# Weight tiles that meet 256 columns: high part 192 bytes further on modulo 256 than the low part

## The chip, the cores and the metric

The kernel runs on one core of one Trainium2 chip. The metric is device time in microseconds (us) of the whole kernel, the median of three runs. TensorE (PE) does the matrix products, and its weight loads are listed apart (PEld); VectorE (DVE) and ScalarE (ACT) do the elementwise work; GpSimd (POOL) does some of it and issues some DMAs; SyncE (SP) issues the rest. All tiles lie in the on-chip memory, 128 partitions high; an address below is a byte offset within each partition.

## The reference

A decoder trunk of two layers over 512 tokens of width 1024, in float32. Each layer is

```python
h = h + 0.5 * swiglu(rmsnorm(h, nw[0]), ffn_w_in[i, 0], ffn_w_out[i, 0])
h = h + mixer(rmsnorm(h, nw[1]))          # layer 0: retention, layer 1: forgetting attention
h = h + 0.5 * swiglu(rmsnorm(h, nw[2]), ffn_w_in[i, 1], ffn_w_out[i, 1])
h = h + sigmoid(rmsnorm(h, nw[3]) @ ple_w_gate[i]) * (p[i] @ ple_w_proj[i])
```

and a last rmsnorm. `swiglu(x)` is `(silu(g) * u) @ w_out` with `g, u` the two halves of `x @ w_in`, and 2816 hidden columns. So there are four such FFNs, two mixers and two gated per-layer inputs (PLE).

## The kernel before

**Products in three parts.** Every float32 operand is held as a high part (`hi`, rounded to the type that TensorE multiplies) and a low part (`lo`, the rest). A product is three matmuls: high by high, high by low, low by high. The weights are the stationary operand, 128 columns of 4 bytes (512 bytes per partition), loaded anew for each matmul; the activations are the moving operand, 512 or 256 columns (2048 or 1024 bytes per partition).

**Two widths.** Most products have 512 moving columns: retention, attention, the FFNs' output matrices and the first PLE (lines 323 to 325 and 702 to 704). With 256 columns run:

- the FFNs' input matrices in a seven-product (Strassen-like) form, line 508. Of the 22 column blocks of an FFN, 20 go this way. A block is seven products of 12 matmuls: eight with the high part (four slices of the weight, each against the high and the low half of an activation), then four with the low part. Two of the seven take the weight as loaded, `pair.t`, a `w8` tile (products `b11` and `t4`); five take sums of its quarters, tiles `s12`, `s34` and `a12`. The order over blocks is: `b11`, two sum products of the next block; then `t4` and three sum products of the one before.
- the other two blocks of each FFN (`plain`, line 543), with `w8` tiles (in the third FFN the first block's come from `s34` and `a12` buffers): high, high, low, then the next tile.
- the second PLE, which runs in two halves of 256 tokens (lines 323 to 325 with 256 columns): high, high, low for each slice of the weight.

An FFN is: two `plain` blocks, then three chunks of 6, 8 and 8 blocks; after each chunk eight output blocks with 512 columns add up. So a chunk's 256-column stretch follows a 512-column one twice per FFN, and follows `plain` once.

**Weights.** A `Weights` object loads each weight by a DMA from SP's queue into a `wraw` buffer, two tiles ahead of use; ACT copies it into the high part, DVE or POOL subtracts to the low part (lines 83, 84), or ACT negates and a DMA of POOL's queue adds (lines 125 to 127). The `w8` tiles have three buffers (`wpool`); for the second PLE a further pool of five (`wkept`) takes the last weights so that both halves can use them. TensorE's order is written out by hand.

**Addresses.** What matters for the change is where the operands of one matmul begin modulo 256 bytes. In the built program:

| buffer | role | begins at, modulo 256 |
|---|---|---|
| `unit_a` to `unit_d` | moving operand of all these products | 32 |
| `w8` in `wpool` (high and low part, 4096 bytes apart) | stationary | 32 |
| `s12`, `s34`, `a12` (all parts) | stationary | 224 |
| `w8` in `wkept` (high and low part) | stationary | 224 |

A slice of a weight begins a multiple of 512 bytes further on, and a half of an activation 1024, so all slices share these values.

Of the kernel before, what the change touches and what calls it, by code (L numbers as in the profile page):

```python
# [12 lines left out]
F32R = mybir.dt.float32r  # L13
# [4 lines left out]
P = 128  # L18
# [9 lines left out]
LOOKAHEAD = 2  # L28
# [7 lines left out]
class Pair:  # L36
# [3 lines left out]
    def __init__(self, ffn, q, r):  # L40
        self.ffn, self.q, self.r, self.direct = ffn, q, r, False
# [13 lines left out]
class Weights:  # L55
# [3 lines left out]
    def __init__(self, tc, raw_pool, pool):  # L59
        self.tc, self.nc, self.raw_pool, self.pool = tc, tc.nc, raw_pool, pool  # L60
        self.plan, self.ready, self.used = [], [], 0
        self.low = self.nc.vector
        self.limit, self.spare = None, []
        self.look, self.placed = LOOKAHEAD, {}
        self.sum_pool, self.open_ffn, self.pairs_used = None, None, 0
        self.ahead, self.behind = 0, ()

# [6 lines left out]
    def load(self, src):  # L74
        raw = self.raw_pool.tile([P, 1024], F32, name="wraw")
        self.nc.sync.dma_start(out=raw[:, : src.shape[1]], in_=src)
        return raw

    def split(self, raw, hi, lo, src=None):
        if self.low is None and src is not None:  # L80
            self.negated(raw, hi, lo, src)
            return
        self.nc.scalar.copy(hi, raw)  # L83
        self.low.tensor_tensor(out=lo, in0=raw, in1=hi.bitcast(F32), op=ALU.subtract)  # L84

    def chunk(self, src):
        n = src.shape[1]
        raw = self.load(src)
        if id(src) in self.placed:
            hi, lo = (t.rearrange("p a c -> p (a c)") for t in self.placed.pop(id(src))())  # L90
            self.split(raw, hi, lo)
            return hi, lo
        if self.spare:
            tiles = [self.spare.pop(0)() for _ in range(4)]
            for i in range(2):
                self.split(raw[:, 512 * i : 512 * (i + 1)], tiles[i], tiles[2 + i])
            return Halves(tiles[0:2]), Halves(tiles[2:4])
        t = self.pool.tile([P, 2, 1024], F32R, name="w8")
        self.split(raw[:, :n], t[:, 0, :n], t[:, 1, :n], src)
        return t[:, 0, :], t[:, 1, :]  # L100

    def emit_parts(self, parts):

        nc = self.nc
        halves = lambda ap: ap.rearrange("p (h c) -> p h c", h=2)
        tiles = [
            (
                self.raw_pool.tile([P, 1024], F32, name="wraw"),
                self.pool.tile([P, 2, 1024], F32R, name="w8"),
            )  # L110
            for _ in range(2)
        ]
        for j0, j1 in parts:
            cs = slice(j0 * P, j1 * P)
            for src, (raw, t) in zip(self.plan, tiles):
                r, hi, lo = (halves(x)[:, :, cs] for x in (raw, t[:, 0, :], t[:, 1, :]))
                nc.sync.dma_start(out=r, in_=halves(src)[:, :, cs])
                nc.vector.tensor_copy(hi, r)
                nc.vector.tensor_tensor(out=lo, in0=r, in1=hi.bitcast(F32), op=ALU.subtract)
            yield  # L120
        self.ready += [(t[:, 0, :], t[:, 1, :]) for _, t in tiles]

    def negated(self, raw, hi, lo, src):

# [4 lines left out]
    def first(self, pair):  # L129

        pair.raw = self.load(pair.q)
        pair.t = self.pool.tile([P, 2, 1024], F32R, name="w8")
        hi, lo = pair.t[:, 0, :], pair.t[:, 1, :]
        if pair.direct:
            self.split(pair.raw, hi, lo)
        else:
            self.negated(pair.raw, hi, lo, pair.q)
# [61 lines left out]
def trunk(ctx, tc, a):  # L199
# [16 lines left out]
    W = Weights(tc, wraw, wpool)  # L216
# [5 lines left out]
    ffn_src = []  # L222
    for i in range(4):
        ins = [Pair(i, a["ffn_w_in"][i, m, 0], a["ffn_w_in"][i, m, 1]) for m in range(NF)]
        chunks = CHUNKS[i]
        outs = [[a["ffn_w_out"][i, m][:, k0 * P : k1 * P] for m in range(KB)] for k0, k1 in chunks]
        for m in [PLAIN[i]] + [k1 + 1 for _, k1 in chunks[:-1]]:
            ins[m].direct = ins[m + 1].direct = True
        ffn_src.append((ins, outs))
    ret_qk = [[a["ret_qk"][c] for c in (2 * h, 2 * h + 1, 8 + 2 * h, 9 + 2 * h)] for h in range(RH)]  # L230
    ret_v = [[a["ret_v"][h][:, c * 1024 : (c + 1) * 1024] for c in range(4)] for h in range(RH)]
    ret_g = [[a["ret_g"][4 * h + c] for c in range(4)] for h in range(RH)]
# [3 lines left out]
    fox_o = [[a["fox_o"][h, c] for c in range(4)] for h in range(2)]  # L236
    ple_g = [[a["ple_gate"][l, m] for m in range(KB)] for l in range(2)]
    ple_p = [[a["ple_proj"][l, c] for c in range(2)] for l in range(2)]

    def plan_ffn(i):  # L240
        ins, outs = ffn_src[i]
        at = PLAIN[i]
        for pair in ins[:at]:
            W.plan += [pair.q, pair.r]
        for (k0, k1), cs in zip(CHUNKS[i], outs):
            upto = min(k1 + 1, NF)
            W.plan += ins[at:upto] + cs
            at = upto
# [61 lines left out]
    def split(src, hi, lo, scale=None):  # L310

        if scale is None:
            high = nc.scalar.copy(hi, src)
            low = nc.vector.tensor_tensor(out=lo, in0=src, in1=hi.bitcast(F32), op=ALU.subtract)  # L314
        else:
            high = nc.scalar.activation(hi, src, AF.Identity, scale=scale)
            low = nc.vector.scalar_tensor_tensor(
                out=lo, in0=src, scalar=scale, in1=hi.bitcast(F32), op0=ALU.mult, op1=ALU.subtract
            )
        return high, low  # L320

    def mm3(out, wh, wl, xh, xl, first, last):
        nc.tensor.matmul(out, wh, xh, start=first, stop=False)  # L323
        nc.tensor.matmul(out, wh, xl, start=False, stop=False)  # L324
        nc.tensor.matmul(out, wl, xh, start=False, stop=last)  # L325
# [18 lines left out]
    class Norm:  # L344
# [9 lines left out]
        def halves(self, b):  # L354
            if self.forms is not None:
                return self.quarters(b)
            hi, lo = self.unit(), self.unit()
            split(h[b], hi, lo, self.gain[:, b : b + 1])
            self.hi.append(hi)
            self.lo.append(lo)  # L360
# [144 lines left out]
    def product(out, w, c, forms, name, first=False):  # L505

        xs = [form[name] for form in forms]
        add = lambda w, x, start, stop: nc.tensor.matmul(  # L508
            out, w, x, start=start, stop=stop, skip_group_check=True
        )  # L510
        for j, (xh, xl) in enumerate(xs):
            wh = w[:, 0, c + j * P : c + (j + 1) * P]
            add(wh, xh, first and j == 0, False)
            add(wh, xl, False, False)
        for j, (xh, xl) in enumerate(xs):
            add(w[:, 1, c + j * P : c + (j + 1) * P], xh, False, j == 3)

    def ffn(i, n, nxt, stack, apool, meanwhile=None):

# [32 lines left out]
        def one(m):  # L552
            pair, g, u = live[m]
            product(g[:, c0], pair.t, 0, n.forms, "b11", True)
            product(g[:, c1], pair.s[0], 0, n.forms, "t1")
# [107 lines left out]
    class OutBoth:  # L663
# [5 lines left out]
        def add(self, i, m):  # L669
            srcs, yhi, ylo = self.parts[i]  # L670
            if (i, m // 2) not in self.ws:
                self.ws[i, m // 2] = W.take(srcs[m // 2])
            wh, wl = self.ws[i, m // 2]
            for k in range(4):
                ks = slice((4 * (m % 2) + k) * P, (4 * (m % 2) + k + 1) * P)
                mm3(self.banks[m], wh[:, ks], wl[:, ks], yhi[k], ylo[k], i == 0 and k == 0, i == 1 and k == 3)
# [560 lines left out]
    norms[4].early = True  # L1237
    first = W.emit_parts(((0, 1), (1, 2), (2, 4)))
    next(first)
    load_x(1, 2)  # L1240
    load_x(2, 4)
# [15 lines left out]
    def ffn_ple(i, l, n, mid, nxt, stack, apool, parts):  # L1257
        phi, plo = [], []

        def load():  # L1260
            pv = a["pT"][l].rearrange("(b p) t -> b p t", p=P)
            for b in range(2):
                t1 = temp()
                nc.sync.dma_start(out=t1, in_=pv[b])
                phi.append(unit(uc))
                plo.append(unit(uc))
                split(t1, phi[b], plo[b])

        ffn(i, n, mid, stack, apool, load)
        stack = open_ffn(i + 1) if i < 3 else None  # L1270
        ple(l, mid, nxt, phi, plo, parts)
        return stack
# [101 lines left out]
```

## Time and profile before

| what | value |
|---|---|
| median of three runs | 2192.59 us (2189.26 to 2194.67) |
| the profiled execution | 2193.35 us, span 2191.5 us |
| mean granted TensorE clock | 0.994 |
| PE busy | 2142.5 us, 98% of the span, 13525 matmuls |
| DVE, ACT, POOL busy | 66%, 55%, 22% |
| matmuls of line 508 / line 543 | 6720 / 768 |

A busy PE is not one at its best: the matmuls overlap, and a duration in the listings runs from an instruction's start to its modelled end. What a matmul costs in a dense stretch is the distance from one start to the next. This is read from the timeline, whose rows give a start in us, a duration, the engine, the line, the operands and the count of equal instructions merged: the difference of two starts over the matmuls in between. In names, `bank<-unit_b,w` is a matmul with moving operand `unit_b` and stationary operand `w8` (the listings cut buffer numbers off, `s12` and `s34` read `s`, `a12` reads `a`).

### The profile page before, as it was taken

Reading aid. Unit: us, or ns where it says so; the run is one execution under the profiler, and the core shown is the slowest. Engines: PE = TensorE matmul, PEld = TensorE weight load, DVE = VectorE, ACT = ScalarE, POOL = GpSimd, SP = SyncE. Lnnn points to the kernel's source line nnn. Section 1 sums busy time; section 2 is a strip of 40 time slices with the busy share of each in tenths; the row PEclk is TensorE's granted clock in tenths of the full one; section 3 lists DMA queues with packets and bytes.
Section 4 is the critical chain, followed back from the end, with each engine's and each line's share of the span. In section 5 each row is a group of like instructions: output and inputs, shape, how many; then the busy total and the mean of one; then the engine's idle time right before and its main releaser. Section 6 shows DMA issues by size and latency. Waiting matters only on the chain.

```text
span 2191.5 us, 34456 instructions
## 1 busy us (share of the span) xinstructions
PE 2142.5 (98%) x13525; PEld 1927.9 (88%) x13525; DVE 1454.5 (66%) x2629; ACT 1202.4 (55%) x2027; POOL 472.6 (22%) x354
## 2 busy tenths in 40 slices
PE   8999999999999999999998999999999999999997
PEld 7999997888888798989988999898788899999987
DVE  8686766352533677767758687775675696777765
ACT  7465553433333574745556556464787774655544
POOL 0010003444344000101142011012334200100055
PEclk9999999999999999999999999999999999999999
DMA  5465562222222244746523555463622144654631
GB/s 174 124 167 148 140 164 97 82 95 77 94 77 87 77 128 132 177 119 152 144 94 97 129 160 149 137 167 105 152 81 88 67 125 114 161 154 139 155 106 40
DMA packets 85315, 267.08 MB, mean 122 GB/s; under 512 B 9360, under 2 KB 12944, under 8 KB 85152
## 3 DMA queue, kind: packets, MB, share of 16 engines
q1 hardware_dynamic: 63328, 209.78, 28.2%
q0 software_dynamic: 20592, 54.01, 14.6%
q8 instruction: 106, 1.74, 0.3%
q10 hardware_dynamic: 1232, 1.09, 0.1%
q14 instruction: 57, 0.47, 0.1%
HBM read 262.71 MB, written 2.13 MB: 121 GB/s over the span
## 4 chain that ended last, share of the span: by engine, by line
PE 85%; DVE 6%; ACT 4%; DMA 2%; issue 2%; POOL 1%; SPq 0%; ACTq 0%; DVEq 0%; POOLq 0%
PE bank L508 33%; PE bank L325 14%; PE bank L323 14%; PE bank L324 13%; PE bank L543 4%; PE bank L703 2%; PE bank L702 2%; PE bank L704 2%; DMA wraw<-in_ffn_w_in 1%; ACT p L1006 1%; DVE w L84 1%; ACT p L1008 1%; ACT w L83 1%; DVE tlo L314 1%; PE bank L337 0%
## 5 line engine op out<-in xcount | busy, mean ns | idle before, releaser
L83 ACT CAST w<-wraw 128x1024 fp32r<-128x1024 f32 (+1 forms) x240 | 243.4, 1021 | 420.0 <-PE bank L325 254.9
L325 PE MATMUL bank<-unit_a,w 128*128 128x512 f32 x736 | 287.2, 390 | 4.3 <-DVE w L84 2.6
L323 PE MATMUL bank<-unit_a,w 128*128 128x512 f32 x736 | 288.5, 392 | 1.9 <-ACT w L83 1.6
L324 PE MATMUL bank<-unit_a,w 128*128 128x512 f32 x736 | 286.7, 390 | 0.2 <-DVE unit_a L314 0.2
L84 POOL TENSOR_TENSOR w<-wraw,w 128x1024 fp32r<-128x1024 f32 x93 | 226.8, 2442 | 259.3 <-ACT w L83 246.8
L83 ACT CAST s<-sums 128x512 fp32r<-128x512 f32 x320 | 191.8, 617 | 153.4 <-DVE sums L157 107.4
L325 PE MATMUL bank<-unit_d,w 128*128 128x512 f32 (+1 forms) x712 | 268.2, 377 | 4.6 <-DVE w L84 4.6
L323 PE MATMUL bank<-unit_d,w 128*128 128x512 f32 (+1 forms) x712 | 269.3, 378 | 3.2 <-ACT w L83 1.6
L324 PE MATMUL bank<-unit_d,w 128*128 128x512 f32 (+1 forms) x712 | 268.0, 376 | 1.8 <-DVE unit_d L314 1.8
L84 DVE TENSOR_TENSOR s<-sums,s 128x512 fp32r<-128x512 f32 x320 | 214.1, 685 | 75.8 <-ACT s L83 75.3
L127 POOL DMA_DIRECT2D a<-in_ffn_w_in x80 | 70.3, 878 | 643.4 <-ACT a L126 422.0
L84 DVE TENSOR_TENSOR w<-wraw,w 128x1024 fp32r<-128x1024 f32 (+1 forms) x147 | 173.3, 1184 | 19.5 <-ACT w L83 19.3
L508 PE MATMUL bank<-unit_b,s 128*128 128x256 f32 x880 | 184.4, 276 | 0.7 <-DVE bank L565 0.7
L508 PE MATMUL bank<-unit_d,s 128*128 128x256 f32 x1140 | 178.4, 276 | 0.0
L508 PE MATMUL bank<-unit_a,s 128*128 128x256 f32 x1260 | 175.0, 276 | 1.4 <-ACT unit_a L387 0.9
L604 DVE SCALAR_TENSOR_TENSOR tmp<-bank,rows 128x512 f32<-128x512 f32 x96 | 66.0, 689 | 164.9 <-PE bank L325 163.7
L325 PEld LDWEIGHTS bank<-unit_a,w 128*128 128x128 f32 x736 | 138.1, 188 | 35.5 <-DVE w L84 4.3
L323 PEld LDWEIGHTS bank<-unit_a,w 128*128 128x128 f32 x736 | 138.2, 188 | 32.2 <-ACT w L83 3.5
L324 PEld LDWEIGHTS bank<-unit_a,w 128*128 128x128 f32 x736 | 138.2, 188 | 28.5 <-DVE unit_a L314 0.5
L325 PEld LDWEIGHTS bank<-unit_d,w 128*128 128x128 f32 x712 | 134.3, 189 | 30.7 <-DVE w L84 6.6
L323 PEld LDWEIGHTS bank<-unit_d,w 128*128 128x128 f32 x712 | 134.4, 189 | 30.2 <-ACT w L83 3.3
L508 PEld LDWEIGHTS bank<-unit_a,s 128*128 128x128 f32 x1260 | 158.0, 188 | 1.8 <-ACT unit_a L387 1.1
(292 smaller groups left out, 4787.9 us busy)
## 6 DMA issues: line engine op xcount, KB each, us to landing
wraw<-in_ffn_w_in SPq DMA_DIRECT2D x174, 512.0 KB, 4.3
wraw<-in_ffn_w_out SPq DMA_DIRECT2D x64, 512.0 KB, 4.7
w<-in_ffn_w_in POOLq DMA_DIRECT2D x56, 512.0 KB, 5.4
a<-in_ffn_w_in POOLq DMA_DIRECT2D x80, 256.0 KB, 6.3
wraw<-in_ffn_w_out SPq DMA_DIRECT2D x32, 384.0 KB, 3.7
wraw<-in_ret_qk SPq DMA_DIRECT2D x16, 512.0 KB, 3.5
wraw<-in_ret_v SPq DMA_DIRECT2D x16, 512.0 KB, 3.6
wraw<-in_ret_g SPq DMA_DIRECT2D x16, 512.0 KB, 3.5
```

The source lines that it names most:

```text
L83: self.nc.scalar.copy(hi, raw)
L84: self.low.tensor_tensor(out=lo, in0=raw, in1=hi.bitcast(F32), op=ALU.subtract)
L127: self.nc.gpsimd.dma_start(out=lo, in_=src, accum_op=ALU.add)
L323: nc.tensor.matmul(out, wh, xh, start=first, stop=False)
L324: nc.tensor.matmul(out, wh, xl, start=False, stop=False)
L325: nc.tensor.matmul(out, wl, xh, start=False, stop=last)
L508: add = lambda w, x, start, stop: nc.tensor.matmul(out, w, x, start=start, stop=stop, skip_group_check=True)
L543: nc.tensor.matmul(o[:, HALVES[t]], x[:, ks], y, start=k == t == q == 0, stop=k == KB - 1 and q == 2, skip_group_check=True,)
L604: nc.vector.scalar_tensor_tensor(out=t1, in0=o, scalar=-0.5, in1=n.r, op0=ALU.mult, op1=ALU.mult)
L702: nc.tensor.matmul(os[t], xh, wh[:, js], start=k == 0, stop=False)
L703: nc.tensor.matmul(os[t], xh, wl[:, js], start=False, stop=False)
L704: nc.tensor.matmul(os[t], xl, wh[:, js], start=False, stop=k == KB - 1)
```

## The change

Tiles for weights in a set `narrow` (the input weights of all four FFNs, and the gate and projection weights of the second PLE) place their high part 48 elements, 192 bytes, into the tile; the low part follows 1024 + 16 elements later. All `w8` tiles get 64 elements (256 bytes) longer, 8448 bytes in place of 8192. By the built program:

| buffer | high, modulo 256 | low, modulo 256 |
|---|---|---|
| `w8` in `wpool`, narrow | 32 -> 224 | 32 -> 32 |
| `w8` in `wkept` (all narrow) | 224 -> 160 | 224 -> 224 |
| `w8` in `wpool`, other | 32 -> 32 | 32 -> 32 |

Buffers that are allocated behind `wpool` move by 768 bytes, so their place modulo 256 stays (modulo 512 it moves by 256). The matmuls whose stationary operand changes its place are 1280 of line 508 (the high parts of `b11` and `t4`), 448 of line 543, and 256 of the second PLE (96 from 32 to 224, 160 from 224 to 160). The instructions of every engine, their order and their waits are the same in both programs: only addresses differ.

```diff
+    def wide(self, src):
+
+        at = 48 if id(src) in self.narrow else 0
+        t = self.pool.tile([P, 2112], F32R, name="w8")
+        return t[:, at : at + 1024], t[:, at + 1024 + (at and 16) :][:, :1024]
...
-        t = self.pool.tile([P, 2, 1024], F32R, name="w8")
-        self.split(raw[:, :n], t[:, 0, :n], t[:, 1, :n], src)
-        return t[:, 0, :], t[:, 1, :]
+        hi, lo = self.wide(src)
+        self.split(raw[:, :n], hi[:, :n], lo[:, :n], src)
+        return hi, lo
...
-        pair.t = self.pool.tile([P, 2, 1024], F32R, name="w8")
-        hi, lo = pair.t[:, 0, :], pair.t[:, 1, :]
+        pair.t = hi, lo = self.wide(pair.q)
...
+    for ins, _ in ffn_src:
+        W.narrow |= {id(x) for pair in ins for x in (pair.q, pair.r)}
...
+    W.narrow |= {id(x) for x in ple_g[1] + ple_p[1]}
...
     def product(out, w, c, forms, name, first=False):
 
         xs = [form[name] for form in forms]
+        both = w if isinstance(w, tuple) else (w[:, 0, :], w[:, 1, :])
...
         for j, (xh, xl) in enumerate(xs):
-            wh = w[:, 0, c + j * P : c + (j + 1) * P]
+            wh = both[0][:, c + j * P : c + (j + 1) * P]
             add(wh, xh, first and j == 0, False)
             add(wh, xl, False, False)
         for j, (xh, xl) in enumerate(xs):
-            add(w[:, 1, c + j * P : c + (j + 1) * P], xh, False, j == 3)
+            add(both[1][:, c + j * P : c + (j + 1) * P], xh, False, j == 3)
```

`emit_parts`, which loads the very first two weights, takes its tiles from `wide` in the same way.

More of the change, by code (lines that the diff above doesn't have):

```diff
@@ L63, in __init__ @@
         self.limit, self.spare = None, []
-        self.look, self.placed = LOOKAHEAD, {}
+        self.look, self.placed, self.narrow = LOOKAHEAD, {}, set()
         self.sum_pool, self.open_ffn, self.pairs_used = None, None, 0
@@ L108, in emit_parts @@
                 self.raw_pool.tile([P, 1024], F32, name="wraw"),
-                self.pool.tile([P, 2, 1024], F32R, name="w8"),
+                *self.wide(src),
             )
-            for _ in range(2)
+            for src in self.plan[:2]
         ]
@@ L114, in emit_parts @@
             cs = slice(j0 * P, j1 * P)
-            for src, (raw, t) in zip(self.plan, tiles):
-                r, hi, lo = (halves(x)[:, :, cs] for x in (raw, t[:, 0, :], t[:, 1, :]))
+            for src, (raw, wh, wl) in zip(self.plan, tiles):
+                r, hi, lo = (halves(x)[:, :, cs] for x in (raw, wh, wl))
                 nc.sync.dma_start(out=r, in_=halves(src)[:, :, cs])
@@ L120, in emit_parts @@
             yield
-        self.ready += [(t[:, 0, :], t[:, 1, :]) for _, t in tiles]
+        self.ready += [(wh, wl) for _, wh, wl in tiles]
     def negated(self, raw, hi, lo, src):
```

## The prediction

> **What bounds the kernel now.** First the page: busy times and the chain of waits.
>
> ```profile
> PE 2142.5 (98%) x13525; PEld 1927.9 (88%) x13525; DVE 1454.5 (66%) x2629; ACT 1202.4 (55%) x2027; POOL 472.6 (22%) x354
> ...
> PE 85%; DVE 6%; ACT 4%; DMA 2%; issue 2%; POOL 1%; SPq 0%; ACTq 0%; DVEq 0%; POOLq 0%
> PE bank L508 33%; PE bank L325 14%; PE bank L323 14%; PE bank L324 13%; PE bank L543 4%; PE bank L703 2%; PE bank L702 2%; PE bank L704 2%; DMA wraw<-in_ffn_w_in 1%; ACT p L1006 1%; DVE w L84 1%; ACT p L1008 1%; ACT w L83 1%; DVE tlo L314 1%; PE bank L337 0%
> ```
>
> TensorE is on 85% of the chain, and line 508 alone, where most of the change lies, on 33%. Two windows inside FFN stretches (columns: length, then busy us of PE, PEld, DVE, ACT, POOL, clock, DMA share, GB/s) show whether anything stands close behind it:
>
> ```profile
> 140.00:200.00 60.00, 60.00 (x520) 59.82 (x519) 49.73 (x91) 44.88 (x79) 9.63 (x11) 1.00 0.73 185
> ...
> 1890.00:1950.00 60.00, 60.00 (x524) 60.00 (x523) 48.20 (x89) 45.23 (x79) 9.65 (x11) 1.00 0.75 188
> ```
>
> PE has no idle there; DVE has 10 us of 60 left, ACT 15, the DMA engines a quarter. So a matmul that takes 1 ns less is 1 ns off the end, and there is room for the 1% that is in question.
>
> Next, the groups of line 508, minimum/median/maximum ns:
>
> ```profile
> L508 PEld LDWEIGHTS bank<-unit_a,s x1260: 186/188/192, 40.9 to 1068.1; 128*128 128x128 f32 x180
> L508 PE MATMUL bank<-unit_a,s x1260: 276/276/387, 41.1 to 1068.2; 128*128 128x256 f32 x180
> ...
> L508 PEld LDWEIGHTS bank<-unit_b,w x720: 186/192/192, 39.5 to 2066.3; 128*128 128x128 f32 x180
> L508 PE MATMUL bank<-unit_b,w x720: 277/283/387, 39.6 to 2066.4; 128*128 128x256 f32 x180
> ```
>
> The same instruction takes 7 ns more with a `w8` tile than with a sum tile, and its weight load 4 ns more. Distances of starts say what it costs:
>
> ```profile
> 194.91 0.88 PE L508 MATMUL bank<-unit_b,w 128*128 128x256 f32 x6
> 195.63 0.40 PE L508 MATMUL bank<-unit_c,w 128*128 128x256 f32 x2
> 195.87 0.52 PE L508 MATMUL bank<-unit_b,w 128*128 128x256 f32 x3
> 196.23 0.28 PE L508 MATMUL bank<-unit_c,w 128*128 128x256 f32 x1
> 196.35 2.88 PE L508 MATMUL bank<-unit_a,s 128*128 128x256 f32 x24
> 199.07 0.40 PE L323 MATMUL bank<-unit_d,w 128*128 128x512 f32 x1
> ```
>
> Twelve with `w8`: 1.44 us, 120.0 ns each. 24 with sum tiles: 2.72 us, 113.3 ns each. I call these the 120 pace and the 113 pace. `w8` begins at 32 modulo 256, like the moving operand, and the sum tiles at 224. That it is the place and not the kind of tile, the second PLE shows, where `w8` tiles stand at both places on the same lines:
>
> ```profile
> 2162.71 0.28 PE L323 MATMUL bank<-unit_c,w 128*128 128x256 f32 x1
> ...
> 2163.43 0.28 PE L323 MATMUL bank<-unit_d,w 128*128 128x256 f32 x1
> ...
> 2166.83 0.59 PE L1220 MATMUL bank<-tmp,ones_r 128*128 128x256 f32 x2
> 2167.08 0.47 PE L323 MATMUL bank<-unit_d,w 128*128 128x256 f32 x1
> 2167.38 0.28 PE L324 MATMUL bank<-unit_d,w 128*128 128x256 f32 x1
> ...
> 2170.45 0.28 PE L323 MATMUL bank<-unit_c,w 128*128 128x256 f32 x1
> ```
>
> The six matmuls from 2162.71 use a `w8` tile at 32: 0.72 us, 120 each. The 30 from 2163.43 use kept tiles at 224: 3.40 us, 113.3 each. But the 26 from 2167.38 also use kept tiles at 224, and take 3.07 us, 118.1 each. So there is a third, 118 pace, at the same addresses. What differs is what came before: the 113 pace began straight behind a run at 120, the 118 pace behind a break. An FFN shows the same:
>
> ```profile
> 54.10 0.85 PE L508 MATMUL bank<-unit_b,s 128*128 128x256 f32 x5 [0.70 <-DVE bank L565]
> ...
> 55.61 1.58 PE L508 MATMUL bank<-unit_a,s 128*128 128x256 f32 x12
> 57.03 0.75 PE L508 MATMUL bank<-unit_b,a 128*128 128x256 f32 x5
> ...
> 58.44 0.87 PE L508 MATMUL bank<-unit_b,w 128*128 128x256 f32 x6
> ...
> 59.87 2.88 PE L508 MATMUL bank<-unit_a,s 128*128 128x256 f32 x24
> 62.59 1.60 PE L508 MATMUL bank<-unit_a,w 128*128 128x256 f32 x12
> ```
>
> A wait at 54.10, then 24 sum-tile matmuls in 2.83 us, 117.9 each; twelve `w8` ones in 1.43 us (119.2); then 24 sum-tile ones in 2.72 us, 113.3. The twelve at 32 moved TensorE from the 118 pace to the 113 pace. My reading, argued and not shown: the load of the next weight and the moving stream read the memory side by side, collide when they meet at the same place modulo 256, and whether they meet depends on both places and on the stream's lead over the load; a run at equal places makes each matmul wait for its weights, and that wait builds the lead with which 224 runs free.
>
> **The change part by part.**
>
> *Line 508, high parts.* 4 FFNs x 20 blocks x 2 products x 8 = 1280 matmuls go from 32 to 224. From 120.0 to 113.3 each saves 6.7 ns: **8.5 us**. This asks that the 113 pace survives the four low matmuls, which stay at 32. For it: a run at 32 is itself the only thing in the trace that starts the 113 pace. If they ran at 118 the gain would be 1280 x 2.1 = 2.7 us.
>
> *Line 508, the entry of a chunk.* Two chunks of each FFN begin behind 512-column matmuls, with `b11`:
>
> ```profile
> 121.41 0.39 PE L325 MATMUL bank<-unit_d,w 128*128 128x512 f32 x1
> 121.63 0.88 PE L508 MATMUL bank<-unit_b,w 128*128 128x256 f32 x6
> ...
> 123.07 2.88 PE L508 MATMUL bank<-unit_a,s 128*128 128x256 f32 x24
> 125.79 0.40 PE L508 MATMUL bank<-unit_a,w 128*128 128x256 f32 x2
> ```
>
> Now twelve at 32 (1.44 us, 120 each) stand first and the 24 behind them are at 113.3 (2.72 us) at once. After the change eight at 224 stand first, behind 512 columns, then only four at 32. What 224 does behind 512 columns, the third FFN's first block shows, whose weights lie in sum buffers:
>
> ```profile
> 1169.18 0.75 PE L543 MATMUL bank<-unit_b,s 128*128 128x256 f32 x5
> ...
> 1172.72 0.40 PE L543 MATMUL bank<-unit_d,s 128*128 128x256 f32 x2
> ```
>
> 30 matmuls in 3.54 us: the 118 pace from the first on. So each entry starts at 118, and the whole result hangs on whether four matmuls at 32 do what twelve did. If the first four do, eight entries lose 8 x 8 x 4.6 = 0.3 us. If they never do, the stretch stays at 118: the slower rival. I take 0.3, because such a run comes twice in each block, each time at another point of the pattern, and one hit suffices.
>
> *Line 543.* 448 high parts, now at 120:
>
> ```profile
> 1199.72 0.88 PE L543 MATMUL bank<-unit_c,w 128*128 128x256 f32 x6
> 1200.44 0.88 PE L543 MATMUL bank<-unit_a,w 128*128 128x256 f32 x6
> ```
>
> Here high, high, low alternate, which no row shows. Bounds: 118 for the high ones saves 448 x 2.1 = 0.9 us, 113.3 saves 3.0; below nothing I exclude, since no row at 224 is above 118. `plain` follows breaks and 512 columns, so I take the lower part, **1.3 us**.
>
> *Second PLE.* 96 high parts go from 32 to 224: 0.2 to 0.6 us saved. 160 high parts of kept tiles go from 224 to 160, because the pool itself begins at 224: there "192 further" doesn't bring them to the place that is known to be good. No row has 160 against 32. Bounds: from 118 to 113.3, 0.7 saved; from 113.3 to 120, 1.1 lost. I take 0 for both together.
>
> *What ACT, DVE and the DMAs write* begins 192 bytes further on and is the same size; DVE's and ACT's idle in the windows above covers a few ns each. The waits of TensorE on weights that are read late stay as they are:
>
> ```profile
> PE bank L325 <- DVE w L84: 7.2, 9, 2.0
> ```
>
> If these nine waits ran by a clock of their own, they would take back what the chunk before gained, at most 4 x 6 blocks x 107 ns = 2.6 us over the four FFNs; the weight buffers are freed by TensorE itself, so I take 0.
>
> Sum: -8.5 + 0.3 - 1.3 = **-9.5 us** against the profiled execution, 2193.35, which lies 0.76 over the median shown: 2192.59 - 9.5 = **2183**.
>
> **A rule that speaks against it.** The rows above have a `w8` load at 192 ns and a sum-tile load at 188, and 120 against 113.3 on the same lines with the place alone different. The Trainium skill, "SBUF — State Buffer", section "Who interferes with whom", gives TensorE two independent read ports, one for the moving operand and one for the weight load, and says "PE and ACT never wait on anyone". By that page no address would matter and the time would stay at 2192.6; the trace does not agree.
>
> **The rivals.**
>
> *The 118 pace stays (slower).* Four matmuls at 32 are too few, and every chunk, once behind 512 columns or a wait, keeps the 118 pace. A block of 84 is now 24 x 120 + 60 x 113.3 = 9.68 us. It would be 76 x 117.9 + 8 x 119.2 = 9.91 us, 0.234 more; 80 blocks: +18.7, less 0.9 of line 543: **2210**. In the forecast a block is 76 x 113.3 + 8 x 120 = 9.57, 0.107 less. So the change turns to a loss when more than 107/341 = 31% of the blocks stay at 118. For it: 224 never goes to 113 by itself, in 24 to 36 matmuls. Against it: the runs at 32, though short.
>
> *Between the two (no change).* With 13% to 50% of the blocks at 118 the time is within 0.3% of before, about 6.6 us, which is what a measurement can tell: **2189**.
>
> *Nothing happens*, because place was not the cause: **2192.6**. The kept tiles speak against it.
>
> *A period of 512 bytes.* All sum tiles move by 768 bytes. If the place counts modulo 512, their 4800 matmuls may fall to 120: +32 us less 8.5, **2216**. No dense stretch of before tells 256 from 512.
>
> **How the numbers follow.** The forecast 0.48, all of it faster by over 0.3%. Between the two 0.17, nothing happens 0.04: same 0.21. The 118 pace 0.28, period of 512 0.03: slower 0.31. The forecast's own range is 2180 (line 543 and the PLE in full) to 2186. To leave out no more than 0.2 I go up to 2209, which takes in the cases between and most of the slower one.
>
> **What would show it.** In the profile after, the timeline of a chunk: eight `unit_b,w` and `unit_c,w` matmuls 113 ns apart, four 120 apart, and sum tiles at 113.3. Median of `w` in line 508 falls from 283 to 276, sum tiles stay at 276. If sum tiles rise to about 279 to 280, the 118 pace has taken hold and I am wrong in sign; if they rise to 283, the period is 512. If `w` stays at 283, place was not the cause. The second PLE from 2143 to 2180 tells what 160 does.

## The result

The change makes the kernel slower: 2203.68 us median (2202.75 to 2206.18) against 2191.1 us of the kernel before beside it (2189.26 to 2194.67), a ratio of 1.0056 with a 95% interval of 1.004 to 1.0071. The forecast was 2183, so it had the sign wrong. The profiled execution took 2206.18 us, its span is 2204.4 us, 12.9 more than before, at a clock of 0.995 (0.994 before).

In the changed file line 508 is 518, 543 is 553, and 323 to 325 are 332 to 334. First the page: busy times and the chain of waits of the kernel after.

```profile
PE 2157.1 (98%) x13525; PEld 1943.6 (88%) x13525; DVE 1456.0 (66%) x2629; ACT 1202.4 (55%) x2027; POOL 471.5 (21%) x354
...
PE bank L518 36%; PE bank L334 13%; PE bank L332 13%; PE bank L333 13%; PE bank L553 3%; PE bank L712 2%; PE bank L713 2%; PE bank L714 2%; DVE w L90 1%; ACT p L1016 1%; ACT p L1018 1%; ACT w L89 1%; DVE tlo L323 1%; DVE acc L456 0%; PE bank L346 0%
```

The same matmuls, the same engines behind them; only PE's busy time has grown, by 14.6 us, and the products' line went from 33% of the chain to 36%. Two windows inside FFN stretches of the kernel after (columns as in the prediction):

```profile
140.00:200.00 60.00, 60.00 (x507) 59.84 (x506) 49.52 (x90) 43.59 (x78) 9.41 (x11) 1.00 0.75 185
...
1900.00:1960.00 60.00, 60.00 (x511) 60.00 (x510) 47.82 (x87) 44.62 (x78) 9.64 (x11) 1.00 0.77 190
```

PE is still without idle, but gets 507 and 511 matmuls into 60 us where it got 520 and 524. The groups of the products (minimum/median/maximum ns), after:

```profile
L518 PE MATMUL bank<-unit_a,s x1260: 276/279/392, 38.4 to 1073.5; 128*128 128x256 f32 x180
...
L518 PE MATMUL bank<-unit_b,w x720: 278/280/386, 37.0 to 2079.1; 128*128 128x256 f32 x180
L518 PEld LDWEIGHTS bank<-unit_c,s x560: 187/188/189, 52.0 to 2080.6; 128*128 128x128 f32 x187
```

`w` fell from 283 ns, but to 280 and not to 276; and the sum tiles, which nobody touched, rose from 276 to 279. That is the sign that the prediction named for its slower rival. The timeline of one block behind the 512 columns that end a chunk, after (start, duration, engine, line, operands, count):

```profile
119.67 0.87 PE L518 MATMUL bank<-unit_b,w 128*128 128x256 f32 x6
...
120.61 0.52 PE L518 MATMUL bank<-unit_b,w 128*128 128x256 f32 x3
120.97 0.28 PE L518 MATMUL bank<-unit_c,w 128*128 128x256 f32 x1
121.09 2.99 PE L518 MATMUL bank<-unit_a,s 128*128 128x256 f32 x24
123.92 1.59 PE L518 MATMUL bank<-unit_a,w 128*128 128x256 f32 x12
...
129.58 0.87 PE L518 MATMUL bank<-unit_b,w 128*128 128x256 f32 x6
```

Eight matmuls at 224 (119.67 to 120.61) take 117.5 ns each, the four at 32 120, and the 24 with sum tiles behind them 2.83 us, 117.9 each, where the kernel before had 113.3. The block takes 9.91 us. It goes on so: of 6080 matmuls at 224 only five start the next one within 114.5 ns, and none of the 160 runs of four at 32 is followed by the 113 pace.

The whole difference of 12.9 us lies on three places. Adding up the distances from each matmul to the next: the products 780.2 us before and 797.4 after (+17.2), the plain products (line 543) 110.5 and 107.1 (-3.4), the second PLE's matmuls of 256 columns 62.2 and 61.3 (-0.9).

### The profile page after: what moved, and what is told of

Read it like the earlier page. It is cut to its first block, busy times and chain, and to the rows that moved or that the text cites. A ratio compares the mean times of both kernels' runs of the same rounds, so it can differ in the third digit from the quotient of the medians.

```text
span 2204.4 us, 34456 instructions
## 1 busy us (share of the span) xinstructions
PE 2157.1 (98%) x13525; PEld 1943.6 (88%) x13525; DVE 1456.0 (66%) x2629; ACT 1202.4 (55%) x2027; POOL 471.5 (21%) x354
## 4 chain that ended last, share of the span: by engine, by line
PE 85%; DVE 8%; ACT 4%; issue 2%; DMA 1%; POOL 1%; SPq 0%; DVEq 0%; ACTq 0%; POOLq 0%
PE bank L518 36%; PE bank L334 13%; PE bank L332 13%; PE bank L333 13%; PE bank L553 3%; PE bank L712 2%; PE bank L713 2%; PE bank L714 2%; DVE w L90 1%; ACT p L1016 1%; ACT p L1018 1%; ACT w L89 1%; DVE tlo L323 1%; DVE acc L456 0%; PE bank L346 0%
## 5 line engine op out<-in xcount | busy, mean ns | idle before, releaser
L518 PE MATMUL bank<-unit_d,s 128*128 128x256 f32 x1140 | 183.3, 279 | 0.0
L518 PE MATMUL bank<-unit_a,s 128*128 128x256 f32 x1260 | 180.3, 279 | 1.3 <-ACT unit_a L396 0.9
L518 PEld LDWEIGHTS bank<-unit_a,s 128*128 128x128 f32 x1260 | 162.5, 188 | 1.7 <-ACT unit_a L396 1.1
```

What stands on the lines that cost most here:

```text
L518: add = lambda w, x, start, stop: nc.tensor.matmul(out, w, x, start=start, stop=stop, skip_group_check=True)
```

## The experiments

In the table, "paced" is the sum of those distances over the 6720 matmuls of the products, where one above 130 ns counts as 115; "waits" is what the longer ones have above 115. Both are from the one profiled execution, the ratio from all. In `abut`, `abut_late` and `order_only` 1.6 us of the "waits" are no waits: 16 matmuls in a row stand 198 to 214 ns apart while the granted clock is 0.5.

| kernel | paced us | waits us | ratio to before, 95% interval |
|---|---|---|---|
| before | 774.5 | 5.7 | |
| the change | 792.4 | 5.0 | 1.0056 [1.004, 1.0071] |
| `ffn_both` | 791.4 | 5.3 | 1.0057 [1.0043, 1.0072] |
| `len_only` | 774.6 | 8.1 | 1.0008 [0.9997, 1.002] |
| `lead_high` | 771.2 | 8.9 | 0.9986 [0.9977, 0.9996] |
| `lead_both` | 768.5 | 10.2 | 0.9987 [0.9976, 0.9999] |
| `ffn_low` | 770.5 | 9.3 | 0.9985 [0.9972, 0.9998] |
| `lead_seven` | 768.1 | 13.9 | 0.9978 [0.9965, 0.9992] |
| `abut` | 767.8 | 14.1 | 0.9992 [0.9984, 1.0001] |
| `abut_late` | 768.5 | 9.3 | 0.9966 [0.9954, 0.9978] |
| `order_only` | 774.6 | 9.1 | 0.9998 [0.9987, 1.0009] |

### The pace by itself

A kernel of nothing but matmuls, no part of the trunk, in segments that begin with eight of 512 columns. The stationary tiles `s_a` to `s_h` begin at 0, 32, 64 and so on to 224 modulo 256, so `s_b` is 32 and `s_h` is 224; `z_b` and `z_h` are the same places 256 bytes on; the moving tile begins at 32.

```diff
+    for c in PLACES:
+        segment((40, c))
+    for c in PLACES:
+        segment((12, "b"), (40, c))
+    for n in (1, 2, 3, 4, 5, 6, 8, 10, 12, 16):
+        segment((24, "h"), (n, "b"), (24, "h"))
```

> No part of the trunk is computed: the kernel runs only matmuls, in segments, and copies the input out. Each segment starts with eight 512-column matmuls, then come runs of 256-column ones. The moving operand begins at 32 modulo 256; the stationary tiles s_a to s_h begin at 0, 32, 64 ... 224 (s_b 32, s_h 224), z_b and z_h at 32 and 224 plus 256. Theory 'memory': behind 512 columns s_h runs at 118 ns, behind twelve at s_b at 113.3; a run of s_b shorter than some number between 4 and 12 leaves s_h at 118, a longer one starts 113.3; once at 113.3, a run of four s_b (120 each) does not end it, and 300 s_h in a row stay at 113.3. Rival 'the short run breaks it': behind twelve s_b and 24 s_h at 113.3, four s_b put the next s_h back to 118. Rival 'period 512': z_b differs from s_b and z_h from s_h; by the period of 256 they are alike. If only the difference of the two places counts, moving at 224 with stationary at 224 runs at 120 and with 160 like s_h.

Its timeline, for 224 straight behind 512 columns, then behind twelve at 32 (a row of `128x512 x20` is eight of 512 and twelve of 256 columns), then with five and with six at 32 in between:

```profile
73.11 4.87 PE L54 MATMUL bank<-mov,s_h 128*128 128x256 f32 x40
77.82 3.46 PE L54 MATMUL bank<-mov,s_b 128*128 128x512 f32 x20
...
137.14 4.70 PE L54 MATMUL bank<-mov,s_h 128*128 128x256 f32 x40
141.67 2.00 PE L54 MATMUL bank<-mov,s_b 128*128 128x512 f32 x8
...
177.55 0.76 PE L54 MATMUL bank<-mov,s_b 128*128 128x256 f32 x5
178.15 2.99 PE L54 MATMUL bank<-mov,s_h 128*128 128x256 f32 x24
180.98 2.03 PE L54 MATMUL bank<-mov,s_b 128*128 128x512 f32 x8
...
185.67 0.88 PE L54 MATMUL bank<-mov,s_b 128*128 128x256 f32 x6
186.39 2.88 PE L54 MATMUL bank<-mov,s_h 128*128 128x256 f32 x24
189.11 2.00 PE L54 MATMUL bank<-mov,s_b 128*128 128x512 f32 x8
```

The same 40 matmuls take 4.71 us (117.8 each) in one place and 4.53 us (113.3 each) in the other. Behind five at 32 the 24 stay at 117.9, behind six they are at 113.3. One to five left 118; 6, 8, 10, 12 and 16 ended it. The other way round it is lighter: out of the 113 pace, a single matmul at 32 dropped the 24 behind it to 117.7 in the one segment that tried it, while 2, 3, 4, 6, 8 and 12 left them at 113.3. The kernel's own pattern (8 at 224, 4 at 32, 32 at 224, 4 at 32, and so on) stayed at 117.6 to 117.8 for three blocks when 512 columns stood ahead, and at 113.3 when twelve at 32 did. So both paces are stable under the change's pattern, and which one a segment has is settled at its entry.

Of the eight places only 224 had the 113 pace against a moving tile at 32; the others took 116.6 to 120.1 each either way. `z_b` read as `s_b` and `z_h` as `s_h`, so the period is 256. With the moving tile at 224, stationary tiles at 160 did 117.8 and, behind twelve at 224, 113.3: in these three cases (with 224 against 224 at 120.0) what counts is the difference of the two places.

### The entry given back

The tiles are as long as the change's, and each FFN block has its own places: `HIGH` is the change's (high parts at 224, low at 32), `BOTH` has both parts at 224, `LOW` is the mirror, `NONE` both at 32 as before. The PLE is as before.

```diff
+LOW, HIGH, BOTH, NONE = (0, 1072), (48, 1088), (48, 1072), (0, 1024)
+FFN_PLACES = lambda m: NONE if m in (0, 1, 2, 7, 15) else HIGH   # lead_high
+FFN_PLACES = lambda m: NONE if m in (0, 1, 2, 7, 15) else BOTH   # lead_both
+FFN_PLACES = lambda m: LOW                                       # ffn_low
...
+        hi, lo = self.places.get(id(src), (0, 1024))
+        t = self.pool.tile([P, 2112], F32R, name="w8")
+        return t[:, hi : hi + 1024], t[:, lo : lo + 1024]
```

Blocks 0 and 1 are plain products; 2, 7 and 15 are those whose `b11` enters a chunk.

> As the changed kernel in line 508 (high part at 224, low at 32), but plain blocks and the blocks 2, 7 and 15 stay at 32 in both parts. Memory theory: the lead starts the 113 pace, the runs of four at 32 do not end it: 17 x 16 x 4 = 1088 high parts save 6.7 ns: about 2184. Rival, the short runs break it: sum tiles back at 118 behind the first four lows, about 2205 like the changed kernel.

In line 508, `lead_high` is the change but for three of an FFN's twenty blocks. Paced, it is 21.2 us under the change, and its time is 2190.68 us, 0.9986 of before [0.9977, 0.9996]. That is some 6 us over the 2184 that was expected: 929 of its matmuls at 224 stayed at 118, and its waits are 3.2 us more than before. Where its runs of four at 32 stand in the 113 pace (113 of 136) they take 120.0 each and leave 113.3 behind them; the 23 that stand in 118 leave 118. That four low matmuls break the 113 pace, the other way to read the loss, is ruled out: they only don't begin it.

> The mirror of the change: FFN input weights have the high part at 32 and the low part at 224; the second PLE is as before. So each product with w8 begins with eight at 32. Memory theory: eight behind 512 columns are enough to start the 113 pace, and the four lows gain 6.7 ns: 640 x 6.7 = 4.3 us less, 2187, and a little less in line 543. Rival, eight are too few: sum tiles at 118, about 2208.

The mirror (`ffn_low`), with eight in a row at 32 in each product, has 113.3 in every chunk, behind an entry too: 2189.65 us, 0.9985 [0.9972, 0.9998]. Paced it gained 4.0 us, near the 4.3 expected; waits took 3.6 of them back.

> FFN input weights have both parts at 224, apart from the plain blocks and the blocks 2, 7 and 15, whose products come first behind another width: these stay at 32 in both parts. The second PLE is as before. Memory theory: the twelve at 32 that lead each stretch start the 113 pace and it lasts to the stretch's end: 17 blocks x 24 x 4 x 6.7 ns = 10.9 us less than before, some of it lost behind waits in the first FFN: about 2181. If the 113 pace ends by itself within tens of matmuls, sum tiles and w8 run at 118: about 2208.

In `lead_both` whole chunks run at 113.3, up to 540 matmuls at 224 without a break, but the time is 2189.95 us, 0.9987 [0.9976, 0.9999]. Paced it gained 6.0 us, not 11, because 1123 of its matmuls at 224 still ran at 118 (the first FFN's first chunk, and what follows a wait in the chunks behind); and 4.5 us came back as waits. The waits of PE, in this kernel:

```profile
PE bank L524 <- ACT tmp L580: 5.7, 5, 2.2
```

and before:

```profile
PE bank L508 <- ACT tmp L564: 2.0, 2, 1.7
```

One of them is the 2.18 us ahead of 1936.05. What stands ahead of it on VectorE and ScalarE (timeline):

```profile
1925.12 0.68 DVE L606 TENSOR_TENSOR tmp<-bank,tmp 128x512 f32<-128x512 f32 x1
1928.15 0.69 DVE L165 TENSOR_TENSOR sums<-wraw 128x512 f32<-128x512 f32 x1 [2.34 <-DMA wraw<-in_ffn_w_in]
...
1935.16 0.43 DVE L578 TENSOR_TENSOR bank<-bank,tmp 128x256 f32<-128x256 f32 x1
...
1935.62 0.37 ACT L580 COPY tmp<-bank 128x256 f32<-128x256 f32 x1 [0.31 <-DVE bank L578]
...
1936.05 0.50 PE L524 MATMUL bank<-unit_b,w 128*128 128x256 f32 x2 [2.18 <-ACT tmp L580]
```

VectorE stood 2.34 us for a weight's load and then worked without idle up to the addition of line 578, for which ScalarE's copy waited, and TensorE for the copy. So this wait hangs on that load; for the others of this kind no such chain was followed.

### No run at 32, and no place moved

```diff
+FFN_PLACES = lambda m: BOTH   # ffn_both
+FFN_PLACES = lambda m: NONE   # len_only
```

> Both parts of all weights of the FFN's narrow products at 224, none at 32: no run at 32 is left in a chunk. Theory: behind the 512 columns that end each chunk nothing brings the 113 pace back, so all 84 matmuls of a block stay at 117.8: in a block 48+32 at 117.8 and not 24 at 120.0 and 60 at 113.3 to 114.3, some 0.21 us by 80 blocks, so 14 to 18 us over the kernel before, 2206 to 2211. Rival (a tile whose two parts have one place is simply the fastest place, 113 to 114 for all): 2178 to 2183. Second rival (the place has no part in it): 2193.

With both parts at 224 in all blocks TensorE never leaves the 118 pace: every dense stretch, the longest of 672 matmuls, has a mean of 117.8. The groups show it (the same columns as above):

```profile
L524 PE MATMUL bank<-unit_a,s x1260: 276/279/387, 38.6 to 1073.8; 128*128 128x256 f32 x180
...
L524 PE MATMUL bank<-unit_b,w x720: 278/280/389, 37.2 to 2081.7; 128*128 128x256 f32 x180
```

The run (`ffn_both`) took 2204.99 us, 1.0057 [1.0043, 1.0072], the same loss as the change's, with no low part left at 32. The place at which every tile stands best is not the best place for all of them.

> Only the length of the change: the tiles are 256 bytes longer, and both parts stay where they were, modulo 256 (32). Theory: the addresses move by multiples of 256 bytes, to which the pace is blind, so the line of the products stays at 780 us and the time within 0.2% of the kernel before (2189 to 2197). Rival (the longer tile alone moves what the splits, the DMAs or a period of 512 bytes see): over 2198.

The longer tiles alone (`len_only`) change nothing that the interval shows: 2194.48 us, 1.0008 [0.9997, 1.002], paced 774.6 us. They shift addresses by 256 bytes and its multiples, so this says of the kernel, too, that 512 has no part in it. It tells something else: its waits are 8.1 us where before had 5.7, with not one matmul faster. So some 2.5 us of "waits" in the table need no explanation by pace.

### More blocks at 32

```diff
+FFN_PLACES = lambda m: NONE if m in (0, 1, 2, 5, 7, 15, 20) else BOTH
```

> Both parts of the FFN's narrow weights at 224, but for seven blocks of each FFN at 32 in both parts: 0, 1, 2, 7 and 15 as in the run with five such blocks, and 5 and 20, which stand right behind the places where a wait had dropped TensorE to 118 again. Theory: a wait or 512 columns end the 113 pace, and a block at 32 brings it back; so the rest of the chunk behind block 5 and block 20 runs at 113 in all three FFNs, and the line of the products falls to some 772 to 776 us (778.7 with five blocks, 780.2 before); the waits for the split stay (5 us where 2 were), so about 2186 to 2189. Rival (the time is set by the DMA of the weights and the split, and faster matmuls only wait longer): the line stays at 778 to 780 and the time at 2190.

The time is where the theory put it, 2188.8 us, 0.9978 [0.9965, 0.9992]; the mechanism is not. Block 5 did bring 113 back in the first FFN's first chunk, but the matmuls at 32 cost 1.3 us more (192 of them by 6.7 ns), paced is 768.1 us as with five blocks, and the line as a whole, 781.9, is over the 772 to 776 that were expected: waits of 13.9 us. The waits of PE in this kernel (`lead_seven`):

```profile
PE bank L524 <- ACT tmp L580: 8.5, 8, 2.0
```

Nor did block 20 always do its part. In the first FFN its `t4`, twelve at 32 with no wait in the 9 us ahead of it, left 118 behind it to the end of the chunk:

```profile
305.16 1.60 PE L524 MATMUL bank<-unit_a,w 128*128 128x256 f32 x12
306.61 0.75 PE L524 MATMUL bank<-unit_b,s 128*128 128x256 f32 x5
...
308.02 1.57 PE L524 MATMUL bank<-unit_a,s 128*128 128x256 f32 x12
```

The twelve take some 120 ns each, the twelve behind them 117.5.

### The change, with its low parts made to stand together

Against the changed kernel only the order of two products is moved: `t4` of a block goes ahead of the next block's `b11`, and `b11` takes its low parts first, so that two runs of four become one of eight.

```diff
+            product(g[:, c0], pair.t, 0, n.forms, "b11", True, True)
-            product(g[:, c0], pair.t, 0, n.forms, "b11", True)
...
+                four(m)
                 if begun < k1:
                     start(begun)
                     one(begun)
                     two(begun)
```

> The change with all its places, and only the order of two products moved: t4 of a block goes ahead of b11 of the next one, and b11 takes its four low parts first, so that two runs of four at 32 stand behind one another as one run of eight in every block. Theory (the pace has a memory: behind 512 columns TensorE stays at 118 for 224, six or more matmuls at 32 in a row bring it to 113, four don't, and a lone one ends 113): the 113 pace is there in nearly all blocks, the line of the products falls by some 8.5 us against the kernel before (780.2 to about 772) and by some 25 us against the change (797.4); with the 4 us that the plain products and the second PLE gain in the change too, and some 4 us of new waits for the split of a weight taken off, about 2182 to 2187. Rival (what the change lost is its longer tiles, their writes or their waits, or two low runs in a block are two too many): it stays by the change, about 2200 to 2206.

Behind 512 columns the pace does what the theory says. The timeline of this kernel (`abut`), behind the 512 columns of the first chunk:

```profile
124.42 1.58 PE L518 MATMUL bank<-unit_a,w 128*128 128x256 f32 x12
125.84 0.52 PE L518 MATMUL bank<-unit_b,w 128*128 128x256 f32 x3
126.19 0.28 PE L518 MATMUL bank<-unit_c,w 128*128 128x256 f32 x1
126.31 0.84 PE L518 MATMUL bank<-unit_b,w 128*128 128x256 f32 x6
126.99 0.39 PE L518 MATMUL bank<-unit_c,w 128*128 128x256 f32 x2
127.22 2.88 PE L518 MATMUL bank<-unit_a,s 128*128 128x256 f32 x24
129.94 0.73 PE L518 MATMUL bank<-unit_b,s 128*128 128x256 f32 x5
```

Eight at 224, eight at 32, and from 126.31 on eight and 24 at 113.3 (0.91 and 2.72 us). All eight chunks that are entered from 512 columns do so, 5593 of 6080 matmuls at 224 run at 113, and paced the products are 24.6 us under the change. The time is 2189.52 us (0.9992, [0.9984, 1.0001]), above the 2182 to 2187 expected, because the order brought waits of its own: in the first block of each FFN `t4` now stands straight behind `t2` and waits for the chain that works on its bank. The longest, in the waits of PE and in the timeline:

```profile
PE bank L518 <- ACT tmp L578: 8.1, 4, 4.8
```

```profile
49.45 2.93 PE L518 MATMUL bank<-unit_a,w 128*128 128x256 f32 x12 [4.80 <-ACT tmp L578]
```

So in the next run (`abut_late`) the first block of each FFN gets the change's order back:

```diff
+                if m > PLAIN[i]:
+                    four(m)
                 if begun < k1:
                     start(begun)
                     one(begun)
                     two(begun)
                     begun += 1
+                if m == PLAIN[i]:
+                    four(m)
```

> The run with the order moved, and one thing else: in the first block of each FFN, where no other products lie between t2 and t4, t4 keeps its place behind the next block's t2. In the run with the order moved, t4 of that block waited for the chain of t2 (5.0, 1.3, 1.3 and 1.2 us, 8.7 together), and the line of the products was 781.9 us; its matmuls without such waits took 767.8 (774.5 before, 792.4 in the change). Theory: the waits go, and four blocks in eighty stay at 118 (some 0.9 us): the line falls to about 774, 6 us under the kernel before and 23 under the change, and the time to 2180 to 2187. Rival (the faster stretches run into the loads and splits of the weights whatever the order): waits of the same size turn up elsewhere, the line stays at 780 to 782, the time at 2188 to 2191.

2187.22 us against 2193.65 beside it: 0.9966 [0.9954, 0.9978], faster than the kernel before, and the lowest ratio of all that ran (its interval overlaps that of `lead_seven`). The four waits are gone, the waits fall from 14.1 to 9.3 us; the line is 777.8 us and not 774, because of new waits of 2.1 and 0.6 us and of the clock. Behind the longer of these two waits lies a stretch with a granted clock of 0.5 (columns as in the prediction):

```profile
59.80:63.20 3.40, 3.40 (x18) 3.40 (x17) 1.91 (x5) 1.21 (x2) 0.02 (x1) 0.50 0.86 213
```

Its 16 matmuls 211 to 214 ns apart are another 1.6 us. The first FFN's first chunk and parts of two others stayed at 118. (These sums are from its profiled execution, 2193.69 us, the slowest of its twelve.)

> The order of the run beside it (t4 ahead of the next block's b11, low parts of b11 first) with the places of the kernel before: both parts of every such weight at 32, tiles still 256 bytes longer. It tells the order's own share apart. Theory: the kernel before is at 113 already behind its twelve matmuls at 32, and stays so with 24 in a row, so the order alone gains nothing in pace: the matmuls of the products without their waits at 774 to 776 us (774.5 before), and the time at 2188 to 2196. Rival (the order moved is the gain by itself, by waits or by a pace of its own): the line falls to 774 as in the run beside it, and the time to 2182 to 2187.

The order without the places (`order_only`) changes nothing that the interval shows: 2193.24 us, 0.9998 [0.9987, 1.0009], paced 774.6. The gain of `abut_late` is the change's own, once a chunk's entry has a run that is long enough.

### What counts: the number, or the point in the pattern

Segments with 20 to 23 at 224 ahead of 3 to 7 at 32; and segments at the 113 pace with a wait for a ScalarE copy (line 65) put in.

```diff
+    for lead in (20, 21, 22, 23):
+        for n in (3, 4, 5, 6, 7):
+            segment((lead, "h"), (n, "b"), (24, "h"))
+    for cols in (64, 128, 256, 512):
+        broken(cols, (36, "h"))
+        for n in (4, 8, 12, 24):
+            broken(cols, (n, "b"), (24, "h"), (n, "b"), (24, "h"))
+            broken(cols, (12, "h"), (n, "b"), (24, "h"), (n, "b"), (24, "h"))
```

> No part of the trunk, only matmuls of 256 columns behind 512-column ones, to settle two points that the runs left open. First: behind 512 columns, 20 to 23 matmuls at 224, then 3 to 7 at 32, then 24 at 224. Theory (it is the number at 32 that counts, six or more): 3, 4 and 5 leave the last 24 at 118, 6 and 7 bring them to 113, whatever the number ahead. Rival (it is the point in a repeating pattern at which the run begins that counts): which lengths do it changes with the number ahead. Second: TensorE at 113, then a wait for a ScalarE copy of the bank (64 to 512 columns, four lengths of wait), then 36 at 224 straight away; or 4, 8, 12 or 24 at 32, then 24 at 224, and the same again; or the same behind 12 at 224. Theory: every wait ends 113, so 36 at 224 run at 117.8; 8 and more at 32 bring 113 back, 4 don't. Rival, from the blocks behind waits in the kernels (24 at 32 straight behind a wait left 118 once, and so did 8 twice): straight behind a wait no length does it for sure, and the same run does it behind 12 matmuls at 224.

The timeline, for six at 32 behind 20 and behind 21:

```profile
50.62 0.87 PE L54 MATMUL bank<-mov,s_b 128*128 128x256 f32 x6
51.33 2.99 PE L54 MATMUL bank<-mov,s_h 128*128 128x256 f32 x24
54.15 2.02 PE L54 MATMUL bank<-mov,s_b 128*128 128x512 f32 x8
...
89.16 0.88 PE L54 MATMUL bank<-mov,s_b 128*128 128x256 f32 x6
89.87 2.88 PE L54 MATMUL bank<-mov,s_h 128*128 128x256 f32 x24
92.59 2.00 PE L54 MATMUL bank<-mov,s_b 128*128 128x512 f32 x8
```

2.82 us for 24 in the first case, 2.72 in the second. Both theories have a part: 3, 4 and 5 never did it, 7 always did, and six did it behind 21 (and 24, above) but not behind 20, 22 or 23. So behind 224 in these segments there is a border that shifts with the point in the pattern, between five and seven, and four lies below it.

A wait ended the 113 pace in 19 of 20 cases where matmuls at 224 followed it straight; the one that kept it had the shortest wait, 0.30 us of idle. Runs of 8, 12 and 24 at 32 brought it back in all 24 segments. A run of four did so straight behind the wait in three of four, and behind twelve at 224 in none of four. Rows with a wait, then four at 32, then 24 at 224:

```profile
333.12 0.74 PE L54 MATMUL bank<-mov,s_b 128*128 128x256 f32 x4 [0.41 <-ACT note L65]
333.70 2.88 PE L54 MATMUL bank<-mov,s_h 128*128 128x256 f32 x24
336.42 0.64 PE L54 MATMUL bank<-mov,s_b 128*128 128x256 f32 x4
...
346.19 1.68 PE L54 MATMUL bank<-mov,s_h 128*128 128x256 f32 x12 [0.41 <-ACT note L65]
347.71 0.64 PE L54 MATMUL bank<-mov,s_b 128*128 128x256 f32 x4
348.18 2.99 PE L54 MATMUL bank<-mov,s_h 128*128 128x256 f32 x24
351.01 0.64 PE L54 MATMUL bank<-mov,s_b 128*128 128x256 f32 x4
```

What stays open is why a longer run does it most times and not every time. In the kernels, out of 118, at the full clock and with no wait among the eight matmuls ahead, none of 183 runs of four was followed by 113, 22 of 24 runs of eight were and 7 of 9 runs of twelve; the segments don't reproduce these failures. In `order_only` 24 at 32 behind a wait in the first chunk left 118 for the 60 behind them, and in `abut_late` eight did so. There the granted clock was 0.5, and 16 of the 24 and all of the eight stood 198 to 214 ns apart; no segment ran at such a clock, so whether it is the reason is not shown. Four are not below the border everywhere either: straight behind a wait they did it in three of four segments above, and in `abut` and `abut_late` 113 followed the four that stand first behind the plain products (whose last matmul is at 32 too) in five of eight cases.

## Why the prediction was wrong

**What bounds the kernel: right.** TensorE had no idle in the windows before and has none after. Of the 12.9 us, the matmuls' own pace is +16.5 (products +18.0, plain products -1.3, PLE -0.1); the rest, -3.6, is waits and stretches with a granted clock of 0.5.

**The three paces and the place: right.** 120, 118 and 113 for the same instruction, by the places modulo 256 and by what came before, came back in the runs. The reading behind it, a weight load and a moving stream that collide at one place, is still only argued; that the difference of the two places decides, and not one place alone, speaks for something between the two.

By the Trainium skill, "SBUF — State Buffer", section "Who interferes with whom", TensorE's two read ports are independent and PE waits on no one. That section of the Trainium skill says nothing of places; read as the prediction reads it, that no address matters, the traces don't agree: `len_only` and `ffn_both` differ in nothing but where tiles begin, and are 0.5% apart by their ratios. That the two ports wait for each other is not shown by that.

**The chunk entry: the step that failed.** "I take 0.3, because such a run comes twice in each block, each time at another point of the pattern, and one hit suffices." There was no hit in 160, so every chunk stayed at 118 from its entry to its end, where the sum had 113.3 behind the first eight. That the point in the pattern has a part was a fair thought: six at 32 depend on it. But four behind a run at 224 did it from no point that ran. The trace of before had nothing shorter than twelve that began the 113 pace; from "twelve do it" the prediction went to "four will, sooner or later". It had named the hinge, and given 0.28 to the side that came true.

**Line 508, high parts, -8.5: not there, by that step.** The matmuls at 32 that became 224 went from 120 to 117.8, not to 113.3, and the 4800 that were at 113.3 went up with them. What the term would have been worth is what `abut_late` has: paced -6.0 against before, the whole -8.5 less what stayed at 118.

**Line 543, -1.3: the pace right, the sum larger.** Its paced matmuls went from a mean of 119.5 to 117.8 ns, by 768 is -1.3, as taken; in the second FFN high, high, low ran at 115.6, 117.2 and 120.4. The other -2.1 are waits and the clock: the first FFN's plain products took 32.1 us before and 29.5 after, and 30.0 in `len_only`, where no place is moved. In this FFN 28 matmuls before and 21 after stood some 213 ns apart, which is 0.7 us of the -2.1; the granted clock was 0.5 for two stretches of 3.4 us before and for one after. So that part does not need the change's places.

**Second PLE, 0: right.** Of the -0.9, -0.7 are waits. 160 kept tiles at 160 run at 118.2, 144 at 32 at 120.2, those at 224 at 116.8.

**Waits that take back what the chunk before gained, 0:** not tested by the change, where nothing got faster. Where it did, they are real: `lead_both`, `lead_seven` and `abut_late` have 3.6 to 8.2 us more of them than before (in `abut_late` 1.6 of it is the clock); `len_only` has 2.4 more with no matmul faster. An estimate from `abut_late`, 0.9966 of before: had the forecast's step held, some 7 us of its 9.5 would have come.

**The slower rival: right in place and mechanism.** A block of 9.91 us was worked out, and 9.91 is what the timeline has. The +18.7 of the products came out as +18.0 of pace and -0.7 of waits; line 543 and the PLE gave 4.3 back, not 0.9, most of it by waits and clock that the rival had no reason to touch. Of the 6.3 us by which 2210 was too high, these are 1.5 and 3.4; the rest is the median of before, 2191.1 in the runs beside the change where 2192.59 stood. "Between the two" did not come up: no chunk switched. (Its bounds were too narrow: by the prediction's own 27.3 us from no block at 118 to all, and -9.5 at none, 11% to 59% lie within 6.6 us of before, not 13% to 50%.) "Nothing happens" and the period of 512 are out by `ffn_both` and by `len_only` and the tiles `z_b`, `z_h`.

## What to carry to other kernels

A matmul's pace can have a memory. Where a trace shows one instruction at two paces, the question is not only which operand is better, but which instruction *brings about* the better pace: the slow matmuls of this kernel were what made the others fast, and improving them one by one took that away. A cheap state that a long run of X begins must be tested with the run length that the change leaves; the trace of before can't extrapolate it. A kernel of bare segments told it for four in one run; that eight and twelve can fail, only the whole kernels showed.

And a gain of 5 to 10 ns a matmul can be eaten by waits that were hidden until then: of the 11 us expected of `lead_both`, 3 arrived.

## What the runs showed of the hardware

- Matmuls of 256 columns run at 120.0, 117.8 or 113.3 ns at a granted clock of 1.00, by the places modulo 256 of both operands and by what ran before. Of eight places against a moving tile at 32, only one (192 further) had the 113 pace at all; the others had means of 116.6 to 120.1.
- Out of 118 and behind a run at 224, three to five matmuls at equal places in a row never brought 113, six did at some points of the pattern, seven always did in the segments; in the kernels eight did so 22 times in 24 and twelve 7 times in 9. Once at 113, runs of 2 to 12 of them didn't end it, but the single one that was tried did, and so did 512 columns, and in the segments every wait of 0.36 us of idle or more with matmuls at 224 behind it.
- Both paces held as long as a stretch lasted: 113.3 over 300 matmuls in a segment and 540 in an FFN, 117.8 over 672.
